# Transposing the merged branches of a decoder layer: fp32 transposes on TensorE against a split first and fp32r matmuls of 128 columns

## The chip, the cores and the metric

The kernel runs on one core of a Trainium2 chip. The metric is device time in microseconds (us), taken as the median of three runs. All times below are us unless ns is written.

## The reference

One layer of a decoder trunk, with 256 positions of 2048 channels. Three branches of width 1024 are computed from the normed input, gated, projected to 2048 channels and merged; a last projection and a norm follow. What matters here is the end of it:

```python
    ys = jnp.stack([y_a, y_b, y_x], axis=2)
    branch = jnp.einsum('bsnc,ncd->bsnd', ys, w_branch)
    gates = jax.nn.sigmoid(gate_logits.reshape(bsz, seq, N_BRANCH, D_MODEL))
    merged = jnp.sum(gates * branch, axis=2)
    out = merged @ w_out
    return x + rms_norm(out, post_g)
```

Inputs and outputs are fp32. The sizes in this part: `y_b` is 256 x 1024, `w_branch` of one branch 1024 x 2048, `merged` 256 x 2048, `w_out` 2048 x 2048.

## The kernel before, in words

Every large product is made from two fp32r parts of each operand: a high part (the value rounded to fp32r) and a low part (the rest). `split_to(hi, lo, src)` (L92 to L94) makes them: ScalarE (ACT) casts the source to the high part (L93), VectorE (DVE) subtracts that from the source (L94). Three matmuls then stand for one: high x high, high x low, low x high (`tm_mm`, L181 to L184). Weights come by DMA in tiles `raw` of 128 x 2048 and are split in halves of 128 x 1024 into `hl`, of which there are four buffers; so the split of one half waits until TensorE (PE) is done with the half four before it.

`tm_quarter` (L220) is the loop over one such tile: for each of its two halves it splits the weights, issues 12 matmuls of 512 columns (2 rows of K x 2 blocks of 128 tokens `tb` x 3 products) and then calls `pump`. PE's order is the order of the program text; DVE and ACT are ordered by a scheduler, and the weight splits carry a priority that puts them ahead. Background work lives in generators in the list `bg[2]`. Each `pump` advances each of them to its next `yield None`.

The place of the change is the last branch, B. The loop at L946 goes over `c`, four chunks of 512 channels of the merged result `mg` (two tiles M, one for each block of 128 tokens, tokens on partitions). A chunk has 4 halves of 12 matmuls into `Bp`. After that DVE multiplies `Bp` by the gate (L952, tile H) and adds it to `mg` (L953, tile M), and `merge_t(c)` (L931) is put in the background. The output projection needs `merged` with channels on partitions, as the stationary operand, so `merge_t` transposes the chunk: it passes two pumps, and then for each half `hf` of the chunk PE makes four transposes (L939: 2 blocks of 128 channels x 2 blocks of tokens) into the PSUM tile `mt`, and at the next pump `split_to` (L942) writes the high and low parts from `mt` to `mm_tile(c)`: ACT casts from PSUM, DVE subtracts from PSUM. Tile `mm_tile(c)` takes the slots H2, H3, U and X0 in turn, which a profile shows as H, U and X. The eight groups of transposes so fall two to a chunk, between the halves of the next chunk and, for the last, between the halves of the first block of the output projection (L973).

`pe.transpose(out, in_, ident)` is a matmul in transpose mode: the data is the stationary operand, the fp32 identity of 128 columns moves.

Of the kernel before, what the change touches and what calls it, by code (L numbers as in the profile page):

```python
# [9 lines left out]
F32 = mybir.dt.float32  # L10
F32R = mybir.dt.float32r
# [7 lines left out]
P = 128  # L19
D = 2048  # L20
T = 256
# [23 lines left out]
def trunk(ctx: ExitStack, tc: tile.TileContext, I, out):  # L45
    nc = tc.nc
    v, a, g, pe = nc.vector, nc.scalar, nc.gpsimd, nc.tensor
# [7 lines left out]
    wk = ctx.enter_context(tc.tile_pool(name="wk", bufs=2))  # L55
# [3 lines left out]
    bup = ctx.enter_context(tc.tile_pool(name="bup", bufs=2, space=PSUM))  # L59
    yp = ctx.enter_context(tc.tile_pool(name="yp", bufs=1, space=PSUM))  # L60
    miscp = ctx.enter_context(tc.tile_pool(name="miscp", bufs=1, space=PSUM))
# [4 lines left out]
    def nm(s):  # L66
        n_[0] += 1
        return f"{s}_{n_[0]}"

    def slot(tag, shape, dt=F32):  # L70
        return big.tile(shape, dt, tag=tag, name=nm(tag))
# [20 lines left out]
    def split_to(hi, lo, src):  # L92
        a.copy(out=hi, in_=src)  # L93
        v.tensor_tensor(out=lo, in0=src, in1=hi.bitcast(F32), op=ALU.subtract)  # L94
# [180 lines left out]
    ident = const.tile([P, P], F32, name="ident")  # L275
# [493 lines left out]
    mg = None  # L769
# [18 lines left out]
    def csl(c):  # L788
        return slice(c * 512, (c + 1) * 512)
# [18 lines left out]
    mg = Lazy()  # L808
# [97 lines left out]
    for bp in range(4):  # L906
# [12 lines left out]
        for i in range(2):  # L919
            d = yB[2 * bp + i]  # L920
# [5 lines left out]
    def mm_tile(i):  # L926
        if i not in mm:
            mm[i] = slot(("H2", "H3", "U", "X0")[i], [P, 4, 2, T], F32R)
        return mm[i]

    def merge_t(c):  # L931
        yield None
        yield None
        for hf in range(2):
            tp = miscp.tile([P, 2, T], F32, tag="misc", name=nm("mt"))
            for i in range(2):
                db = c * 4 + hf * 2 + i
                for tb in range(2):
                    pe.transpose(tp[:, i, tb * P:(tb + 1) * P], mg[tb][:, db * P:(db + 1) * P], ident)  # L939
            yield None  # L940
            d = mm_tile(c)[:, 2 * hf:2 * hf + 2]
            split_to(d[:, :, 0], d[:, :, 1], tp)  # L942
            if hf == 0:
                yield None

    for c in range(4):  # L946
        Bp = acc_tile()
        for kq in range(2):
            tm_quarter([Bp[:, 0], Bp[:, 1]], load(I["w_br"][1, c, kq]), yBs, kq, 8)
        for tb in range(2):  # L950
            d = sgB[tb][:, csl(c)]
            v.tensor_tensor(out=d, in0=Bp[:, tb], in1=d, op=ALU.mult)  # L952
            v.tensor_tensor(out=mg[tb][:, csl(c)], in0=mg[tb][:, csl(c)], in1=d, op=ALU.add)  # L953
        bg[2].append(merge_t(c))
# [65 lines left out]
    for tb in range(2):  # L1020
# [3 lines left out]
        c = slice(tb, tb + 1)  # L1024
# [107 lines left out]
```

## Time and profile before

| | |
|---|---|
| device time, median of 3 runs (lowest to highest) | 917.44 us (916.76 to 918.68) |
| the profiled execution, its own time | 916.64 us |
| its span, first to last instruction | 914.9 us |
| PE busy in the span | 902.5 us (99%) |
| DVE busy | 776.6 us (85%) |
| ACT busy | 535.6 us (59%) |
| mean granted clock of PE | 0.999 of full speed |

PE means TensorE's matmuls, PEld its weight loads, which run beside matmuls. A row names line, engine and operation, then out<-in with partitions x elements. Matmuls are pipelined: a row's duration (about 0.38 us for 512 columns) is longer than the step from its start to the start of the next (0.22 us), and what a matmul costs in a stream is that step. An fp32 operation is recorded as `f32` whether it is plain fp32 or fp32r on PE. A plain fp32 matmul shows as two records, a transpose or an fp32r matmul as one.

### The profile page before, as it was taken

The numbers are of one execution on the slowest core, as the hardware profiler recorded it, in microseconds if no ns is written. First come the engines' busy times: TensorE is split into PE (matmuls) and PEld (weight loads), VectorE is DVE, ScalarE is ACT, GpSimd is POOL, SyncE is SP. The second block draws the span as 40 slices with busy tenths as digits, with TensorE's granted clock in tenths as the row PEclk, the third lists the DMA queues.
The fourth block names the chain that finished last, engine by engine and source line by source line (L and its number), as shares of the span: only waits on it lengthen the run. The fifth ranks groups of instructions, "written<-read, shape, count | busy, mean of one in ns | idle before, by whom it ended". The sixth has DMA issues, their size and how long they took to land. (4 is left out here: it accounts for less than half of the span.)

```text
span 914.9 us, 13213 instructions
## 1 busy us (share of the span) xinstructions
PE 902.5 (99%) x4992; PEld 802.5 (88%) x4992; DVE 776.6 (85%) x1324; ACT 535.6 (59%) x865; POOL 22.1 (2%) x46
## 2 busy tenths in 40 slices
PE   9999999999999999999999999999999999999996
PEld 7999998899888888888899888888888888998896
DVE  7899957986779999999897799999998977876554
ACT  8576555665456657475554566555765646544452
POOL 1000000000000000000000000000000000000000
PEclk9999999999999999999999999999999999999999
DMA  9888565556355566655655545556466566657542
GB/s 358 312 318 297 196 226 191 193 190 230 138 190 190 195 223 221 220 204 185 230 190 184 198 184 194 196 200 226 158 234 229 176 207 227 218 184 277 192 177 92
DMA packets 30465, 193.35 MB, mean 211 GB/s; under 512 B 3905, under 2 KB 4417, under 8 KB 8641
## 3 DMA queue, kind: packets, MB, share of 16 engines
q1 hardware_dynamic: 28288, 186.18, 56.7%
q0 software_dynamic: 1536, 4.20, 1.4%
q10 hardware_dynamic: 576, 2.12, 0.6%
q8 instruction: 39, 0.64, 0.3%
q14 instruction: 26, 0.21, 0.1%
HBM read 190.39 MB, written 2.10 MB: 210 GB/s over the span
## 5 line engine op out<-in xcount | busy, mean ns | idle before, releaser
L94 DVE TENSOR_TENSOR hl<-raw,hl 128x1024 fp32r<-128x1024 f32 x319 | 388.1, 1219 | 101.2 <-ACT hl L93 98.1
L93 ACT CAST hl<-raw 128x1024 fp32r<-128x1024 f32 x319 | 329.5, 1045 | 179.9 <-PE acc L184 113.6
L172 PE MATMUL acc<-x,hl 128*128 128x512 f32 x736 | 241.5, 382 | 0.5 <-DVE x L166 0.5
L171 PE MATMUL acc<-x,hl 128*128 128x256 f32 x690 | 189.6, 275 | 0.8 <-DVE hl L94 0.6
L182 PE MATMUL acc<-hl,x 128*128 128x512 f32 x448 | 171.4, 383 | 0.0
L183 PE MATMUL acc<-hl,x 128*128 128x512 f32 x448 | 169.8, 379 | 0.0
L184 PE MATMUL acc<-hl,x 128*128 128x512 f32 x448 | 169.8, 379 | 0.0
L172 PEld LDWEIGHTS acc<-x,hl 128*128 128x128 f32 x736 | 136.8, 189 | 18.4 <-ACT hl L93 1.2
L171 PEld LDWEIGHTS acc<-x,hl 128*128 128x128 f32 x690 | 132.3, 192 | 3.5 <-DVE hl L94 2.4
L182 PEld LDWEIGHTS acc<-hl,x 128*128 128x128 f32 x448 | 84.7, 189 | 13.7 <-issue 2.5
L184 PEld LDWEIGHTS acc<-hl,x 128*128 128x128 f32 x448 | 84.7, 189 | 12.0
L183 PEld LDWEIGHTS acc<-hl,x 128*128 128x128 f32 x448 | 84.7, 189 | 11.3
L182 PE MATMUL acc<-hl,H 128*128 128x512 f32 (+1 forms) x224 | 83.5, 373 | 0.0
L183 PE MATMUL acc<-hl,H 128*128 128x512 f32 (+1 forms) x224 | 83.3, 372 | 0.0
L184 PE MATMUL acc<-hl,H 128*128 128x512 f32 (+1 forms) x224 | 83.2, 372 | 0.0
L183 PEld LDWEIGHTS acc<-hl,H 128*128 128x128 f32 x224 | 42.4, 189 | 5.6 <-DVE hl L94 0.2
L184 PEld LDWEIGHTS acc<-hl,H 128*128 128x128 f32 x224 | 42.4, 189 | 5.5
L182 PEld LDWEIGHTS acc<-hl,H 128*128 128x128 f32 x224 | 42.4, 189 | 5.3
L372 DVE TENSOR_TENSOR p<-p,E 128x512 f32<-128x512 f32 x64 | 44.1, 689 | 1.0
L600 DVE TENSOR_TENSOR_SCAN p<-s5r,p 128x256 f32<-128x256 f32 x64 | 42.5, 683 | 0.9
L372 DVE TENSOR_TENSOR p<-bu,E 128x512 f32<-128x512 f32 x64 | 41.3, 682 | 2.2 <-PE bu L561 2.2
L541 ACT COPY E<-ebase 128x64 f32<-128x64 f32 x32 | 7.7, 245 | 54.1 <-DVE p L372 52.2
(249 smaller groups left out, 1278.4 us busy)
## 6 DMA issues: line engine op xcount, KB each, us to landing
raw<-w_gate SPq DMA_DIRECT2D x48, 1024.0 KB, 4.7
raw<-w_br SPq DMA_DIRECT2D x24, 1024.0 KB, 4.7
raw<-w_out SPq DMA_DIRECT2D x16, 1024.0 KB, 4.7
raw<-w_xq SPq DMA_DIRECT2D x8, 1024.0 KB, 5.1
raw<-wk SPq DMA_DIRECT2D x8, 1024.0 KB, 4.9
raw<-wv SPq DMA_DIRECT2D x8, 1024.0 KB, 4.8
raw<-w_xg SPq DMA_DIRECT2D x8, 1024.0 KB, 4.7
raw<-w_av SPq DMA_DIRECT2D x8, 1024.0 KB, 4.7
```

Of the source, the lines that this page charges most:

```text
L93: a.copy(out=hi, in_=src)
L94: v.tensor_tensor(out=lo, in0=src, in1=hi.bitcast(F32), op=ALU.subtract)
L171: pe.matmul(ps[:, 0:T], lhsT=wl, rhs=hl.moving(0), start=False, stop=False)
L172: pe.matmul(ps, lhsT=wh, rhs=hl.moving_both(), start=first, stop=last)
L182: pe.matmul(ps, lhsT=hl.stationary(0, tb), rhs=two(wh), start=first, stop=False)
L183: pe.matmul(ps, lhsT=hl.stationary(0, tb), rhs=two(wl), start=False, stop=False)
L184: pe.matmul(ps, lhsT=hl.stationary(1, tb), rhs=two(wh), start=False, stop=last)
L372: v.tensor_tensor(out=o, in0=i0, in1=i1, op=op)
L541: a.copy(out=E[:, :, HT:HT + NB], in_=base[:, q])
L600: v.tensor_tensor_scan(out=p2[:, ri], data0=rb, data1=p1[:, ri], initial=0.0, op0=ALU.mult, op1=ALU.add)
```

## The change

`merge_t` splits first and transposes afterwards. When the chunk is merged, `split_to` makes the high and low parts of the 128 x 512 slice for each block of tokens, tokens on partitions, in a new tile `m2` (tag w0). After two pumps PE transposes both parts with plain `pe.matmul`, the data stationary in fp32r and an fp32r copy of the identity (`identr`, made once by ACT) moving, 128 columns: eight matmuls for each half `hf` of the chunk, the high parts into one PSUM tile, the low parts into another. Both come from the pool `bup` (2 buffers), which the kernel before uses for the state-space part and for the last output block, instead of `miscp` (1 buffer). At the next pump ACT copies the first tile to the high part of `mm_tile(c)` and DVE copies the second to the low part.

```diff
+    identr = wk.tile([P, P], F32R, tag="w2", name="identr", padded_shape=[P, 2 * P])
+    a.copy(out=identr, in_=ident)
+
     def merge_t(c):
+        ms_ = []
+        for tb in range(2):
+            m2 = wk.tile([P, 2, 512], F32R, tag="w0", name=nm("m2"))
+            split_to(m2[:, 0], m2[:, 1], mg[tb][:, csl(c)])
+            ms_.append(m2)
         yield None
         yield None
         for hf in range(2):
-            tp = miscp.tile([P, 2, T], F32, tag="misc", name=nm("mt"))
-            for i in range(2):
-                db = c * 4 + hf * 2 + i
-                for tb in range(2):
-                    pe.transpose(tp[:, i, tb * P:(tb + 1) * P], mg[tb][:, db * P:(db + 1) * P], ident)
+            d = mm_tile(c)[:, 2 * hf:2 * hf + 2]
+            tps = []
+            for z in range(2):
+                tp = bup.tile([P, 2, T], F32, tag="bu", name=nm("mt"))
+                for i in range(2):
+                    db = hf * 2 + i
+                    for tb in range(2):
+                        pe.matmul(tp[:, i, tb * P:(tb + 1) * P], lhsT=ms_[tb][:, z, db * P:(db + 1) * P], rhs=identr,
+                                  start=True, stop=True)
+                tps.append(tp)
             yield None
-            d = mm_tile(c)[:, 2 * hf:2 * hf + 2]
-            split_to(d[:, :, 0], d[:, :, 1], tp)
+            a.copy(out=d[:, :, 0], in_=tps[0])
+            v.tensor_copy(out=d[:, :, 1], in_=tps[1])
             if hf == 0:
                 yield None
```

The order of PE at the first group, which transposes the first half of chunk 0 between the third and the fourth half of chunk 1. Before:

```order
L183 MATMUL acc_7532<-hl_7567,yB_7252 128x512
L184 MATMUL acc_7532<-hl_7567,yB_7252 128x512
L939 MATMUL mt_7582<-ident,M_294_2727 128x128
L939 MATMUL mt_7582<-ident,M_295_2729 128x128
L939 MATMUL mt_7582<-ident,M_294_2727 128x128
L939 MATMUL mt_7582<-ident,M_295_2729 128x128
L182 MATMUL acc_7532<-hl_7587,yB_7253 128x512
```

With the change (`m_986` and `m_987` are the two split tiles):

```order
L183 MATMUL acc_7534<-hl_7575,yB_7252 128x512
L184 MATMUL acc_7534<-hl_7575,yB_7252 128x512
L950 MATMUL mt_7591<-identr,m_986_7552 128x128
L950 MATMUL mt_7591<-identr,m_987_7555 128x128
L950 MATMUL mt_7591<-identr,m_986_7552 128x128
L950 MATMUL mt_7591<-identr,m_987_7555 128x128
L950 MATMUL mt_7596<-identr,m_986_7552 128x128
L950 MATMUL mt_7596<-identr,m_987_7555 128x128
L950 MATMUL mt_7596<-identr,m_986_7552 128x128
L950 MATMUL mt_7596<-identr,m_987_7555 128x128
L182 MATMUL acc_7534<-hl_7601,yB_7253 128x512
```

The group keeps its place and has eight matmuls where it had four.

The order of DVE after chunk 0, where the merged result is written and, with the change, split. Before:

```order
L952 TENSOR_TENSOR H_837_6471<-acc_7463,H_837_6471 128x512
L94 TENSOR_TENSOR hl_7587<-raw_7565,hl_7587 128x1024
L953 TENSOR_TENSOR M_294_2727<-M_294_2727,H_836_6470 128x512
L953 TENSOR_TENSOR M_295_2729<-M_295_2729,H_837_6471 128x512
L94 TENSOR_TENSOR hl_7612<-raw_7610,hl_7612 128x1024
L94 TENSOR_TENSOR hl_7632<-raw_7610,hl_7632 128x1024
L94 TENSOR_TENSOR hl_7651<-raw_7649,hl_7651 128x1024
L94 TENSOR_TENSOR H_991_7602<-mt_7582,H_991_7602 128x2x256
```

With the change:

```order
L965 TENSOR_TENSOR H_837_6471<-acc_7465,H_837_6471 128x512
L94 TENSOR_TENSOR hl_7601<-raw_7573,hl_7601 128x1024
L966 TENSOR_TENSOR M_294_2727<-M_294_2727,H_836_6470 128x512
L966 TENSOR_TENSOR M_295_2729<-M_295_2729,H_837_6471 128x512
L94 TENSOR_TENSOR hl_7625<-raw_7623,hl_7625 128x1024
L94 TENSOR_TENSOR m_986_7552<-M_294_2727,m_986_7552 128x512
L94 TENSOR_TENSOR m_987_7555<-M_295_2729,m_987_7555 128x512
L94 TENSOR_TENSOR hl_7656<-raw_7623,hl_7656 128x1024
L94 TENSOR_TENSOR hl_7675<-raw_7673,hl_7675 128x1024
L955 CAST H_991_7590<-mt_7596 128x2x256
```

Two subtractions of 128 x 512 stand between two weight splits, and the subtraction that read `mt` has become a cast. ACT's casts of `m` stand in the same place of its own order.

## Rows read from the trace of the kernel before

**Rows 1.** The page: busy time of the engines, share of the span, instructions; and the granted clock in 40 equal slices of the span.

```profile
PE 902.5 (99%) x4992; PEld 802.5 (88%) x4992; DVE 776.6 (85%) x1324; ACT 535.6 (59%) x865; POOL 22.1 (2%) x46
PEclk9999999999999999999999999999999999999999
```

**Rows 2.** Busy time in the stretch from 786.4 to 842.4, which holds the eight groups of transposes. Columns: busy us and instructions of each engine, PE's granted clock, DMA share, GB/s.

```profile
786.40:842.40 56.00, 56.00 (x277) 50.20 (x276) 39.11 (x45) 25.50 (x29) 0.00 (x0) 1.00 0.62 226
```

**Rows 3.** The chain of work that ended last, in the same stretch: start, length, what. By line the transposes are 6.2% of it.

```profile
by line: PE acc L184 31.6%; PE acc L182 31.3%; PE acc L183 31.2%; PE mt L939 6.2%
796.55 0.44 PE mt L939 x4
...
835.92 0.44 PE mt L939 x4
```

**Rows 4.** PE in order of time (start, length of the row, instructions) around the first and the last group of transposes; 30 matmuls of 512 columns start between 789.70 and 796.17, counting the one at 789.70.

```profile
789.70 0.38 PE L184 MATMUL acc<-hl,yB 128*128 128x512 f32 x1
...
796.17 0.38 PE L184 MATMUL acc<-hl,yB 128*128 128x512 f32 x1
796.39 0.60 PE L939 MATMUL mt<-ident,M 128*128 128x128 f32 x4
796.74 0.47 PE L182 MATMUL acc<-hl,yB 128*128 128x512 f32 x1
797.05 0.38 PE L183 MATMUL acc<-hl,yB 128*128 128x512 f32 x1
...
835.75 0.60 PE L939 MATMUL mt<-ident,M 128*128 128x128 f32 x4
```

**Rows 5.** PE in order of time where fp32r matmuls of 256 columns follow each other, each with its own weight load (L177 to L179); 20 steps lie between the two rows.

```profile
90.73 0.28 PE L177 MATMUL acc<-H,hl 128*128 128x256 f32 x1
...
92.97 0.28 PE L179 MATMUL acc<-H,hl 128*128 128x256 f32 x1
```

**Rows 6.** PE in order of time: four plain fp32 matmuls of 128 columns, outside of transpose mode (L857, two records each), behind a pair of 256 and 512 columns.

```profile
462.50 0.27 PE L171 MATMUL acc<-x,hl 128*128 128x256 f32 x1
462.61 0.38 PE L172 MATMUL acc<-x,hl 128*128 128x512 f32 x1
462.83 1.05 PE L857 MATMUL z<-H,H 128*128 128x128 f32 x8
463.64 0.36 PE L171 MATMUL acc<-x,hl 128*128 128x256 f32 x1
463.83 0.38 PE L172 MATMUL acc<-x,hl 128*128 128x512 f32 x1
```

**Rows 7.** PE in order of time: four transposes whose stationary operand is read with a stride of two elements (L735, `p[:, qb, mb::2]`).

```profile
188.49 0.63 PE L735 MATMUL tp<-ident,p 128*128 128x128 f32 x4
188.88 0.46 PE L172 MATMUL acc<-x,hl 128*128 128x512 f32 x1
189.18 0.27 PE L174 MATMUL acc<-x,hl 128*128 128x256 f32 x1
```

**Rows 8.** Groups of weight loads, shapes kept apart: busy us, mean ns of one. L182 and L178 load fp32r, L857 plain fp32, L625 32 columns, L939 and L735 the data to be transposed.

```profile
L182 PEld LDWEIGHTS acc<-hl,H 128*128 128x128 f32 x224 | 42.4, 189 | 5.3
L178 PEld LDWEIGHTS acc<-H,hl 128*128 128x128 f32 x128 | 24.6, 192 | 0.0
L857 PEld LDWEIGHTS z<-H,H 128*128 128x128 f32 x32 | 4.2, 192 | 0.1
L939 PEld LDWEIGHTS mt<-ident,M 128*128 128x128 f32 x32 | 4.0, 141 | 0.8
L625 PEld LDWEIGHTS y<-s,cb 128*32 128x32 f32 x128 | 3.3, 109 | 3.9 <-issue 2.6
L735 PEld LDWEIGHTS tp<-ident,p 128*128 128x128 f32 x16 | 2.5, 200 | 0.0
```

**Rows 9.** Who waited for whom in the stretch from 786.4 to 842.4: us in total, times, longest.

```profile
ACT hl L93 <- PE acc L184: 31.2, 21, 1.5
DVE hl L94 <- ACT hl L93: 14.9, 12, 1.4
DVE H L952 <- PE acc L184: 0.3, 1, 0.3
```

**Rows 10.** DVE and ACT in order of time from the end of chunk 0 to the first group of transposes and what follows it (start, length, instructions, idle time before).

```profile
791.15 1.28 DVE L953 TENSOR_TENSOR M<-M,H 128x512 f32<-128x512 f32 x2
792.49 1.23 DVE L94 TENSOR_TENSOR hl<-raw,hl 128x1024 fp32r<-128x1024 f32 x1
795.08 1.23 DVE L94 TENSOR_TENSOR hl<-raw,hl 128x1024 fp32r<-128x1024 f32 x1 [1.36 <-ACT hl L93]
797.66 1.23 DVE L94 TENSOR_TENSOR hl<-raw,hl 128x1024 fp32r<-128x1024 f32 x1 [1.36 <-ACT hl L93]
...
791.41 1.05 ACT L93 CAST hl<-raw 128x1024 fp32r<-128x1024 f32 x1 [1.54 <-PE acc L184]
794.00 1.05 ACT L93 CAST hl<-raw 128x1024 fp32r<-128x1024 f32 x1 [1.54 <-PE acc L184]
```

**Rows 11.** Groups of splits of 128 x 512, from SBUF (`hl<-H`) and from PSUM (`H<-mt`): busy us, mean ns of one.

```profile
L94 DVE TENSOR_TENSOR hl<-H,hl 128x512 fp32r<-128x512 f32 x8 | 5.4, 681 | 0.0
L93 ACT CAST hl<-H 128x512 fp32r<-128x512 f32 x8 | 4.8, 603 | 0.0
L94 DVE TENSOR_TENSOR H<-mt,H 128x512 fp32r<-128x512 f32 x4 | 2.7, 683 | 0.0
L93 ACT CAST H<-mt 128x512 fp32r<-128x512 f32 x4 | 2.3, 578 | 0.0
```

## The prediction

> **What bounds the kernel now.** I first read the page's busy times: PE is busy 99% of the span, DVE 85%, ACT 59%, and the granted clock is full in all slices [rows 1]. A share of 99% says PE is the suspect, not that every instruction on it counts, so I went to the stretch of the change. From 786.4 to 842.4 PE is busy for all 56.00 us, DVE for 39.11 and ACT for 25.50 [rows 2], and the chain that ended last is there made of PE alone, the transposes 6.2% of it, in eight pieces of 0.44 us [rows 3]. The waits say the same from the other side: ACT's weight splits wait 31.2 us for PE to release a buffer, DVE's wait 14.9 us for ACT, and PE is in no row as the one that waits [rows 9]. So any time put on PE here is added to the kernel, and any time put on DVE and ACT is free until PE has to wait for it.
>
> The next thing to read is what a matmul costs in this stream. Not its duration: a transpose lasts 273 ns by its record, but four of them and a 512-column matmul pass from 796.39 to 797.05, in 0.66 us [rows 4]. Between 789.70 and 796.17 lie 30 steps of a 512-column matmul, 0.2157 each. So a group of four transposes costs 0.66 - 0.216 = 0.44. A longer base gives it better: first and last group start at 796.39 and 835.75, seven periods of 5.623, each with 24 matmuls of 512 columns (5.177); what is left is 0.446 for a group, 0.1115 for one transpose.
>
> **What is removed.** 32 transposes in 8 groups, 8 x 0.446 = 3.57 us of PE, all on the path.
>
> **What is added on PE.** 64 fp32r matmuls of 128 columns, each with a weight load of 128 x 128. The trace has no fp32r matmul under 256 columns, so its price is bounded. From below: in a pair of 256 and 512 columns the 256 take one step of 0.11 [rows 6], so 128 columns that only stream would take half of it, 0.055; nothing excludes that from the side of the columns, but a matmul can't be cheaper than its stream. From above: a plain fp32 matmul of 128 columns outside of transpose mode takes two records. Eight records and one of 256 columns fill 462.83 to 463.83, so a record is (1.00 - 0.11) / 8 = 0.111 and the matmul 0.223 [rows 6].
>
> Between these I take the weight load as the limit. Where fp32r matmuls of 256 columns follow each other, 20 steps take 2.24 us, 0.112 each [rows 5], where in a pair, with a longer matmul to hide the load, they take 0.11 [rows 6]: as dear, or a touch dearer. A load of 128 columns lasts 189 to 192 ns, one of 32 columns 109 [rows 8]: 96 columns more cost 80 to 83 ns, so 128 columns occupy some 0.11 us of the load path, with a latency on top. That loads can set the step is seen at the other transposes: those of L735 have the same shape as ours, but their strided loads take 200 ns instead of 141 [rows 8], and four of them cost 189.18 - 188.49 - 0.216 = 0.47, so 0.118 each instead of 0.1115 [rows 7]. The new loads are contiguous fp32r, like L178, so I take 0.1115: half as many columns, the same step. 64 x 0.1115 = 7.14 us.
>
> The sum on PE is 7.14 - 3.57 = **+3.57 us**: the work is doubled and the single piece stays as dear as it was. With the step between 0.109 and 0.118 it is 3.4 to 4.0.
>
> The skill speaks against leaving transpose mode at all: the Trainium skill, "TensorE: Matmul & The Clock Gate", section Terms, calls this mode four times faster for FP32. Taken as a rule for these matmuls it would make each 4 x 0.1115 and add 25 us. The trace disagrees even for plain fp32, where the factor is 0.223 / 0.1115 = 2 [rows 4, 6], and the sum goes by the rows.
>
> **What is added on DVE and ACT.** Per chunk DVE gains two subtractions of 128 x 512 from SBUF at 0.68; its two subtractions from PSUM become casts from PSUM, for which the old 0.68 is the nearest row. ACT gains two casts of 0.60 and keeps two copies of 0.58 [rows 11]. Over four chunks DVE goes from 39.1 to 44.5, ACT from 25.5 to 30.3, in a stretch that PE stretches from 56.0 to 59.6. I cost this at nothing; the cover is DVE's idle time behind ACT (1.36 before a weight split [rows 10]) and the four weight buffers. If the cover were gone, up to 5.4 us of DVE work would stand before weight splits.
>
> **The new wait.** PE's groups now wait for the splits. DVE has the merged chunk at 792.43, then a weight split to 793.72, then the two new subtractions to about 795.08, just where the next weight split starts today [rows 10], so that one isn't delayed. ACT is free at 792.46 and done with both casts by 793.66, before its next weight split at 794.00. PE wants the high parts at 796.17 (load one step ahead) and the low parts four matmuls later, at about 796.6 [rows 4]. The slack is 2.5 and 1.5 us. Behind a waiting load stand all further matmuls. The identity is copied once, long before. The copies out of PSUM have the same two pumps as before, and no longer depend on each other; the two `bup` buffers are wanted again only a period of 5.6 us later. No DMA is added or moved past another.
>
> **The number.** The profiled execution took 916.64 us (span 914.9), 0.8 under the median. It should become 920.2; from the median, 917.44 + 3.57 = **921.0 us**. With the bounds of the step and the spread of the runs (0.7 below to 1.2 above) this case gives 920.1 to 922.7. A measurement tells about 0.2%, 1.8 us, from no change, so this is a small but clear loss.
>
> **Rivals.**
>
> *The load path is not the limit (no change).* If fp32r loads can overlap more than these rows show, 128 columns go at their stream, at best 0.055: 64 x 0.055 = 3.52, a difference of -0.05, 917.4. For it: no row has a load behind a shorter matmul. Against: the 0.112 of [rows 5] and the 0.118 of [rows 7], where the step is longer than the columns need. It decides for "same" when the step is under about 0.083 (919.2). I give 0.13, half on each side of that. The Trainium skill, "TensorE: Matmul & The Clock Gate", section Back-to-back issue gap, gives about 81 ns for a stream of loads and matmuls of 128 columns. By it the estimate is 64 x 0.081 - 3.57 = +1.6, 919.1; no run here shows it, as its loads would have to be faster than those of [rows 8].
>
> *Small fp32r matmuls are as dear as fp32.* Then each costs 0.216 to 0.223, the price of 512 columns or of a plain fp32 matmul of 128: +10.3 to +10.7, 927.7 to 928.1. For it: no row under 256 columns in fp32r. Against: 256 and 512 columns of fp32r go at one price per column, without a sign of a fixed cost [rows 4, 5]. Chance 0.10.
>
> *The split comes late.* If DVE takes the next weight split before the two subtractions, they end at 795.08 + 1.23 + 1.36 = 797.67, some 1.0 us after PE wants the low parts, at each of four chunks: 4 us more, 925. It decides when they slip by over 1.5 us. Against: the order has them ahead of that split. Chance 0.09.
>
> That is 0.66 for the forecast, 0.13, 0.10, 0.09, and 0.02 for a gain that no row explains. The range 919.0 to 926.0 holds the forecast, the late split and the nearer half of the first rival: 0.66 + 0.09 + 0.06 = 0.81. Slower by over 0.2%: 0.66 + 0.10 + 0.09 + 0.06 = 0.91; within it 0.07; faster 0.02.
>
> **What would show it.** A group of eight should take 0.89 us from its first start, less the step of the 512 that closes it, where four took 0.446; the period between groups should go from 5.62 to 6.07. The loads of L950 should last 189 to 192 ns, not 141. The clock should stay full, PE should have no idle in the stretch, and the splits of `m` should end before 796. A group of 0.45 would mean the first rival, one of 1.7 the second, and PE idle ahead of L950 with DVE as releaser the third. A time off by more than 1.5 us with groups of 0.89 would mean something outside of `merge_t`, and my sum would be wrong in its cover.

## The result and the profile after

The changed kernel takes 920.96 us (median of 6 runs, 920.76 to 921.85) against 917.96 of the kernel before in the same count of runs. The ratio is 1.0037, with a 95% interval of 1.0027 to 1.0047: slower by 2.5 to 4.3 us (the medians alone are 3.0 apart). The forecast was 921.0 with a range of 919.0 to 926.0.

The page of the changed kernel: busy time of the engines and the granted clock, to be read beside [rows 1].

```profile
PE 906.8 (99%) x5024; PEld 806.6 (88%) x5024; DVE 781.4 (85%) x1332; ACT 539.9 (59%) x874; POOL 22.0 (2%) x46
PEclk9999999999999999999999999999999999999998
```

PE has 32 records more and 4.3 us of busy time more. The granted clock is the same but for the last slice, 8 tenths for 9; there PE runs out of work, its last matmul ending 7.9 us before the end in both kernels. DVE and ACT have grown by 4.8 and 4.3 us. That the numbers are alike means nothing; the chain says which of them counts. The chain of work that ended last, in the stretch from 786 to 846, beside [rows 3]:

```profile
by line: PE acc L182 29.9%; PE acc L183 29.5%; PE acc L184 29.5%; PE mt L950 11.2%
797.37 0.84 PE mt L950 x8
...
839.94 0.84 PE mt L950 x8
```

It is still PE alone, and the share of the transposing matmuls has gone from 6.2% to 11.2%. PE in order of time around the first and the last group, beside [rows 4]:

```profile
796.99 0.38 PE L184 MATMUL acc<-hl,yB 128*128 128x512 f32 x1
797.21 1.00 PE L950 MATMUL mt<-identr,m 128*128 128x128 f32 x8
798.05 0.44 PE L182 MATMUL acc<-hl,yB 128*128 128x512 f32 x1
798.33 0.38 PE L183 MATMUL acc<-hl,yB 128*128 128x512 f32 x1
...
839.77 1.00 PE L950 MATMUL mt<-identr,m 128*128 128x128 f32 x8
```

Eight matmuls and one of 512 columns pass from 797.21 to 798.33. Less 0.216 for the 512, a group costs 0.904. The long base says the same: (839.77 - 797.21) / 7 = 6.080 a period, less 5.177 for 24 matmuls of 512 columns, is 0.903. One matmul's share of the price is 0.113. (The eight starts alone fill 797.21 to 798.05, 0.105 each; the rest of the price is that the 512-column matmul behind them takes 0.28 to its successor instead of 0.216.) The weight loads of these matmuls, beside those of [rows 8]:

```profile
L950 PEld LDWEIGHTS mt<-identr,m 128*128 128x128 f32 x64 | 8.4, 191 | 0.4
```

They last 191 ns on average, like the fp32r loads of [rows 8] (189 to 192), where the transposes' loads lasted 141. The waits from 786.4 to 846.4, beside [rows 9], have no row in which PE waits, and neither have those of any run below:

```profile
ACT hl L93 <- PE acc L184: 30.7, 21, 2.0
DVE hl L94 <- ACT hl L93: 12.5, 12, 1.7
DVE H L965 <- PE acc L184: 1.9, 4, 0.5
```

And DVE in order of time before the first group, beside [rows 10]: the two new subtractions fill the gap in which DVE had waited for ACT.

```profile
791.98 1.29 DVE L966 TENSOR_TENSOR M<-M,H 128x512 f32<-128x512 f32 x2
793.31 1.23 DVE L94 TENSOR_TENSOR hl<-raw,hl 128x1024 fp32r<-128x1024 f32 x1
794.45 1.29 DVE L94 TENSOR_TENSOR m<-M,m 128x512 fp32r<-128x512 f32 x2
795.90 1.23 DVE L94 TENSOR_TENSOR hl<-raw,hl 128x1024 fp32r<-128x1024 f32 x1 [0.16 <-ACT hl L93]
```

The idle time before the next weight split has shrunk from 1.36 to 0.16 us. The low parts are there at 795.74. The first load of the group starts with the matmul at 796.99, and the low parts are wanted four matmuls later.

One thing has to be kept out of the comparison: the span of this profiled execution is 919.4 against 914.9, 4.5 longer. Of that, 0.8 lies before the change begins to act: the first group starts 0.82 later than before. In the first 14 us ACT waited 0.6 longer for loads of the input; the rows there are, before and after:

```profile
ACT x L165 <- DMA st<-start: 0.9, 3, 0.4
```

```profile
ACT x L165 <- DMA st<-start: 1.5, 2, 1.2
```

The code there is the same in both, and I take this for the spread between executions: in the traces of the runs below the first group starts anywhere from 796.77 to 798.69. From the first group on the difference is 3.66 = 8 x 0.457, which is the change.

### The profile page after: what moved, and what is told of

Its sections match the earlier page's. It is cut to its first block, busy times and chain, and to the rows that moved or that the text cites. A ratio compares the mean times of both kernels' runs of the same rounds, so it can differ in the third digit from the quotient of the medians.

```text
span 919.4 us, 13303 instructions
## 1 busy us (share of the span) xinstructions
PE 906.8 (99%) x5024; PEld 806.6 (88%) x5024; DVE 781.4 (85%) x1332; ACT 539.9 (59%) x874; POOL 22.0 (2%) x46
## 5 line engine op out<-in xcount | busy, mean ns | idle before, releaser
L182 PE MATMUL acc<-hl,x 128*128 128x512 f32 x448 | 171.4, 383 | 0.0
L182 PEld LDWEIGHTS acc<-hl,x 128*128 128x128 f32 x448 | 84.7, 189 | 13.7 <-issue 2.5
L182 PE MATMUL acc<-hl,H 128*128 128x512 f32 (+1 forms) x224 | 83.4, 373 | 0.0
L182 PEld LDWEIGHTS acc<-hl,H 128*128 128x128 f32 x224 | 42.4, 189 | 5.3
```

The lines of the kernel that those rows point to most:

```text
L182: pe.matmul(ps, lhsT=hl.stationary(0, tb), rhs=two(wh), start=first, stop=False)
```

## The experiments

The theory: PE's own work is the whole loss; each fp32r matmul of 128 columns costs one weight load, 0.112, and half as many columns gain nothing. The rivals: short fp32r matmuls have a price of their own; or part of the loss is the new work on DVE and ACT. A group's price is read in each run as above, from the row of the group to the second matmul behind it, less 0.216. Starts are shown to 0.01 us, so such a price is uncertain by about 0.01 (the kernel before gives 0.444 so, and 0.447 over the seven periods of [rows 3]).

**Half a load.** Stationary operand of 64 columns, POOL fills the channels that are left out.

```diff
-                        pe.matmul(tp[:, i, tb * P:(tb + 1) * P], lhsT=ms_[tb][:, z, db * P:(db + 1) * P], rhs=identr,
+                        pe.matmul(tp[0:64, i, tb * P:(tb + 1) * P], lhsT=ms_[tb][:, z, db * P:db * P + 64], rhs=identr,
                                   start=True, stop=True)
...
-            a.copy(out=d[:, :, 0], in_=tps[0])
-            v.tensor_copy(out=d[:, :, 1], in_=tps[1])
+            g.memset(d[64:P].bitcast(F32), 0.0)
+            a.copy(out=d[0:64, :, 0], in_=tps[0][0:64])
+            v.tensor_copy(out=d[0:64, :, 1], in_=tps[1][0:64])
```

> The changed kernel with a weight load of 64 columns in place of 128 for each of the 64 matmuls (the transposed copy of the other 64 channels of each block is left out and filled with zeros by POOL). Moving columns stay at 128. Theory that the load path sets the step: a load of half the columns takes about 0.055, the step of the eight matmuls falls from 0.113 to 0.055 to 0.065, a group from 0.91 to about 0.5, and the time by 8 x 0.4 = 3.2, to about 917.8, near the kernel before. Rival, that short fp32r matmuls have a price of their own (half the rate under 256 columns, or a floor): step 0.11, group 0.9, time 921.0 as with the change.

Measured: 918.96 us, ratio to the kernel before 1.0011 (1.0002 to 1.0020). PE in order of time:

```profile
798.34 0.64 PE L950 MATMUL mt<-identr,m 128*64 128x128 f32 x8
798.82 0.44 PE L182 MATMUL acc<-hl,yB 128*128 128x512 f32 x1
799.10 0.38 PE L183 MATMUL acc<-hl,yB 128*128 128x512 f32 x1
```

The group costs 799.10 - 798.34 - 0.216 = 0.54 instead of 0.90, and eight starts fill 798.34 to 798.82, 0.06 each where the change has 0.105. So a matmul of 128 fp32r columns has no floor at 0.11: with a shorter load it goes at 0.06. That is the theory's side, if a little above the expectation in the group (0.5) and in the time (917.8). The loads:

```profile
L950 PEld LDWEIGHTS mt<-identr,m 128*64 128x64 f32 x64 | 5.1, 135 | 0.8
```

64 columns less take 191 - 135 = 56 ns off the record, so 128 columns are worth an estimated 112 ns: the step of the change. Half a load also halves what a matmul writes to PSUM; the next run does that too, and gains nothing by it.

**Half the moving columns.** 64 columns of the identity, loads as with the change; POOL fills the tokens that are left out.

```diff
-                        pe.matmul(tp[:, i, tb * P:(tb + 1) * P], lhsT=ms_[tb][:, z, db * P:(db + 1) * P], rhs=identr,
+                        pe.matmul(tp[:, i, tb * P:tb * P + 64], lhsT=ms_[tb][:, z, db * P:(db + 1) * P], rhs=identr[:, 0:64],
                                   start=True, stop=True)
...
```

> The changed kernel with 64 moving columns in place of 128 (half of the identity; the other tokens of each block are left out and filled with zeros by POOL). The weight loads stay at 128 columns. Theory that the load path sets the step: step 0.11, group 0.9, time 921.0, nothing gained by half the columns. Rival, that the columns set it at half the rate of long matmuls: step 0.055, group 0.45, time about 917.5.

Measured: 920.9 us, ratio 1.0038 (1.0025 to 1.0051), as with the change.

```profile
796.87 0.97 PE L950 MATMUL mt<-identr,m 128*128 128x64 f32 x8
797.67 0.47 PE L182 MATMUL acc<-hl,yB 128*128 128x512 f32 x1
797.98 0.38 PE L183 MATMUL acc<-hl,yB 128*128 128x512 f32 x1
```

The group costs 0.894, so nothing is gained by half the columns.

**Twice the moving columns.** The identity beside zeros, 256 columns, the two token blocks summed in PSUM.

```diff
...
-                        pe.matmul(tp[:, i, tb * P:(tb + 1) * P], lhsT=ms_[tb][:, z, db * P:(db + 1) * P], rhs=identr,
-                                  start=True, stop=True)
+                        pe.matmul(tp[:, i, :], lhsT=ms_[tb][:, z, db * P:(db + 1) * P],
+                                  rhs=identr[:, 1 - tb:3 - tb, :], start=tb == 0, stop=tb == 1)
```

> The changed kernel with 256 moving columns in each of the 64 matmuls (the identity beside zeros, the two token blocks added up in PSUM): twice the columns, the same loads. Theory that the load path sets the step at up to 256 columns: step 0.112, group 0.9, time 921.0, nothing lost by twice the columns. Rival, that the columns count in any part: step up to 0.22, time up to 928.

Measured: 921.09 us, ratio 1.0036 (1.0022 to 1.0049).

```profile
796.77 1.12 PE L951 MATMUL mt<-identr,m 128*128 128x256 f32 x8
797.73 0.38 PE L182 MATMUL acc<-hl,yB 128*128 128x512 f32 x1
797.94 0.38 PE L183 MATMUL acc<-hl,yB 128*128 128x512 f32 x1
```

The group costs 0.954. Four times the columns of the run before raise it by 7%. Together the three runs show that the load sets the step: half the load takes a matmul's share of the price from 0.113 to 0.068, while 64, 128 and 256 columns give 0.112, 0.113 and 0.119.

**The split alone.** The kernel before with DVE's and ACT's new splits added, unused.

```diff
     def merge_t(c):
+        for tb in range(2):
+            m2 = wk.tile([P, 2, 512], F32R, tag="w0", name=nm("m2"))
+            split_to(m2[:, 0], m2[:, 1], mg[tb][:, csl(c)])
         yield None
```

> The kernel before, with the split of the merged chunk on DVE and ACT added and not used; the transposes are those of before. DVE gets 5.5 us of work more in this stretch, ACT 4.9. Theory that all of this is under cover: as before, 918.0, within 0.6, and no wait of PE in the stretch. Rival, that part of the loss comes from DVE and ACT and their weight splits: up to 3 us over before, with PE idle ahead of L182 to L184 in the stretch.

Measured: 917.43 us, ratio 1.0001 (0.9992 to 1.0009). The group as before:

```profile
798.00 0.60 PE L942 MATMUL mt<-ident,M 128*128 128x128 f32 x4
798.36 0.47 PE L182 MATMUL acc<-hl,yB 128*128 128x512 f32 x1
798.67 0.38 PE L183 MATMUL acc<-hl,yB 128*128 128x512 f32 x1
```

798.67 - 798.00 - 0.216 = 0.454, within the rounding of before, and no row of the waits has PE in it. The cover holds, to within 0.8 us.

**High parts alone.** Half of the changed kernel's matmuls; the low part is a second copy of the high one.

```diff
-            for z in range(2):
+            for z in range(1):
...
-            v.tensor_copy(out=d[:, :, 1], in_=tps[1])
+            v.tensor_copy(out=d[:, :, 1], in_=tps[0])
```

> The changed kernel with the high parts alone transposed, 32 fp32r matmuls in place of 64; the low part is copied from the same PSUM tile, so DVE and ACT do as much as with the change. Theory that a transpose costs the same step in either form and only the count matters: group 0.45, period of groups 5.62, time as before, 918.0, within 0.6. Rival, that the fp32r form has a cost of its own beside the count (a turn from one form to the other, or the waits on the split): over before by 1 us or more.

Measured: 918.06 us, ratio 1.0002 (0.9993 to 1.0011).

```profile
797.73 0.56 PE L950 MATMUL mt<-identr,m 128*128 128x128 f32 x4
798.13 0.44 PE L182 MATMUL acc<-hl,yB 128*128 128x512 f32 x1
798.40 0.38 PE L183 MATMUL acc<-hl,yB 128*128 128x512 f32 x1
```

Four fp32r matmuls cost 0.454, within 0.01 of four fp32 transposes, with as much work on DVE and ACT as with the change. The loss is the count.

**The old transposes with half a load.** The other half of the channels is filled by POOL. This is to see whether they cost the same as the new matmuls for the same reason.

```diff
-                    pe.transpose(tp[:, i, tb * P:(tb + 1) * P], mg[tb][:, db * P:(db + 1) * P], ident)
+                    pe.transpose(tp[0:64, i, tb * P:(tb + 1) * P], mg[tb][:, db * P:db * P + 64], ident)
...
```

> The kernel before, its 32 fp32 transposes with a load of 64 columns in place of 128 (the other 64 channels of each block are left out and filled with zeros by POOL). Theory: an fp32 transpose is bound by its moving columns, at two units each, not by its load, so the step stays 0.109, group 0.44, time 918.0. Rival: these too are bound by the load: step 0.055, group 0.25, time 916.4.

Measured: 917.47 us, ratio 0.9997 (0.9988 to 1.0007).

```profile
796.83 0.60 PE L939 MATMUL mt<-ident,M 128*64 128x128 f32 x4
797.19 0.47 PE L182 MATMUL acc<-hl,yB 128*128 128x512 f32 x1
797.49 0.38 PE L183 MATMUL acc<-hl,yB 128*128 128x512 f32 x1
```

The group stays at 0.444. The fp32 transpose isn't held by its load. The 0.111 a record in [rows 6] can't say whether it is held by its columns, as each of those records has a load of 128 columns too. Plain fp32 matmuls of 256 columns in the kernel before can:

```profile
178.91 1.89 PE L714 MATMUL sc<-M,X 128*128 128x256 f32 x8
180.44 0.46 PE L171 MATMUL acc<-x,hl 128*128 128x256 f32 x1
180.74 0.38 PE L172 MATMUL acc<-x,hl 128*128 128x512 f32 x1
```

Eight records and one fp32r matmul of 256 columns fill 178.91 to 180.74, so a record of 256 fp32 columns takes (1.83 - 0.11) / 8 = 0.215, twice what 256 fp32r columns take, and 128 of them an estimated 0.108. The 0.109 of the transposes fits that. So the two forms seem to meet at 0.11 by coincidence, one by its columns, the other by its load; no run varies the columns of the fp32 transposes.

**The change in transpose mode.** The same 64 pieces, fp32r, with `pe.transpose`.

```diff
-                tp = bup.tile([P, 2, T], F32, tag="bu", name=nm("mt"))
+                tp = bup.tile([P, 2, T], F32R, tag="bu", name=nm("mt"))
...
-                        pe.matmul(tp[:, i, tb * P:(tb + 1) * P], lhsT=ms_[tb][:, z, db * P:(db + 1) * P], rhs=identr,
-                                  start=True, stop=True)
+                        pe.transpose(tp[:, i, tb * P:(tb + 1) * P], ms_[tb][:, z, db * P:(db + 1) * P], identr)
...
```

> The changed kernel with its 64 matmuls in transpose mode on the fp32r parts (PSUM tile fp32r). The loads of transposes lasted 141 ns before, those of the change 189 to 192. Theory: the load path sets the step of the change, and transpose mode loads about twice as fast, so the step falls to what 128 columns need, about 0.06, a group to about 0.52, the time to about 918.2, the loss nearly gone. Rival: fp32r in transpose mode moves at the fp32 transposes' rate (0.109): group 0.9, time 921.0.

Measured: 920.04 us, ratio 1.0020 (1.0011 to 1.0029). Loads, then PE in order of time:

```profile
L950 PEld LDWEIGHTS mt<-identr,m 128*128 128x128 f32 x64 | 6.3, 140 | 0.8
```

```profile
798.69 0.80 PE L950 MATMUL mt<-identr,m 128*128 128x128 f32 x8
799.33 0.46 PE L182 MATMUL acc<-hl,yB 128*128 128x512 f32 x1
799.62 0.38 PE L183 MATMUL acc<-hl,yB 128*128 128x512 f32 x1
```

The loads take 140 ns as expected, but the group costs 0.714, not 0.52, and eight starts fill 0.64, 0.08 each. My expectation missed: transpose mode gives back less than half of the loss. The loads of one group in order of time, with the change and here:

```profile
797.00 1.07 PEld L950 LDWEIGHTS mt<-identr,m 128*128 128x128 f32 x8
```

```profile
798.48 0.87 PEld L950 LDWEIGHTS mt<-identr,m 128*128 128x128 f32 x8
```

The first load has a whole 512-column matmul to itself. From the second on, the single loads in the trace start 0.109 to 0.112 apart with the change and 0.082 to 0.091 apart here, while the first two matmuls of a group here are 0.06 to 0.07 apart and the later ones fall into the loads' step. So the load seems to be the limit here too, at 0.085 and not at the 0.06 that I took from the duration of its record. That is read from the starts; no run varies the load in this mode.

**The low part in bf16.** A second piece of type bf16 in place of the low fp32r one, with a bf16 identity; the low part has fewer bits.

```diff
...
-            m2 = wk.tile([P, 2, 512], F32R, tag="w0", name=nm("m2"))
-            split_to(m2[:, 0], m2[:, 1], mg[tb][:, csl(c)])
+            m2 = wk.tile([P, 512], F32R, tag="w0", name=nm("m2"), padded_shape=[P, 1024])
+            m3 = wk.tile([P, 512], BF16, tag="w1", name=nm("m3"), padded_shape=[P, 1024])
+            split_to(m2, m3, mg[tb][:, csl(c)])
...
-                        pe.matmul(tp[:, i, tb * P:(tb + 1) * P], lhsT=ms_[tb][:, z, db * P:(db + 1) * P], rhs=identr,
+                        pe.matmul(tp[:, i, tb * P:(tb + 1) * P], lhsT=ms_[tb][z][:, db * P:(db + 1) * P], rhs=idents[z],
```

> The changed kernel with the low part kept and transposed in bf16 (bf16 identity), so 32 of the 64 loads are bf16, like the warm-up's at 140 ns; the low part loses bits. Theory that the load path sets the step: fp32r 0.112 and bf16 about 0.06, group 4 x 0.112 + 4 x 0.06 = 0.69, time about 918 + 8 x (0.69 - 0.447) = 919.9, a good 1 us under the change. Rival, that each matmul of 128 columns costs 0.11 whatever its type: 921.0.

Measured: 919.99 us, ratio 1.0020 (1.0011 to 1.0028). Loads by type, then PE in order of time:

```profile
L954 PEld LDWEIGHTS mt<-identr,m 128*128 128x128 f32 x32 | 4.8, 191 | 0.4
L954 PEld LDWEIGHTS <-m 128*128 128x128 bf16 x32 | 1.8, 98 | 0.0
```

```profile
797.15 0.56 PE L954 MATMUL mt<-identr,m 128*128 128x128 f32 x4
797.55 0.40 PE L954 MATMUL mt<-identb,m 128*128 128x128 bf16 x4
797.76 0.47 PE L182 MATMUL acc<-hl,yB 128*128 128x512 f32 x1
798.07 0.38 PE L183 MATMUL acc<-hl,yB 128*128 128x512 f32 x1
```

The group costs 0.70, as expected: four fp32r matmuls fill 797.15 to 797.55, 0.10 each, and the rest of the group, four bf16 ones, takes 0.30: their starts fill 797.55 to 797.76, 0.05 each, and the rest is the turn back to fp32r. The same 128 columns are cheaper where the load is shorter, here by type and not by leaving data out; the moving identity changes its type as well.

**All groups in one table.** Eight times a group's price, less eight times 0.447, against the measured ratio as a difference at 918 us. The fourth column is uncertain by about 0.1.

| run | matmuls in a group | group, us | 8 x (group - 0.447) | measured, us (95%) |
|---|---|---|---|---|
| the change | 8 | 0.904 | 3.7 | 3.4 (2.5 to 4.3) |
| half a load | 8 | 0.54 | 0.7 | 1.0 (0.2 to 1.8) |
| half the columns | 8 | 0.894 | 3.6 | 3.5 (2.3 to 4.7) |
| twice the columns | 8 | 0.954 | 4.1 | 3.3 (2.0 to 4.5) |
| split alone | 4 | 0.454 | 0.1 | 0.1 (-0.7 to 0.8) |
| high parts alone | 4 | 0.454 | 0.1 | 0.2 (-0.6 to 1.0) |
| old ones, half a load | 4 | 0.444 | 0.0 | -0.3 (-1.1 to 0.6) |
| transpose mode, fp32r | 8 | 0.714 | 2.1 | 1.8 (1.0 to 2.7) |
| low part in bf16 | 8 | 0.70 | 2.0 | 1.8 (1.0 to 2.6) |

PE's price of a group accounts for each of the nine times, within its interval. None of them is clearly faster than the kernel before.

## Why the prediction was right

- *PE is the bound in this stretch.* Right, and for the reason given: no PE wait in the rows, and the nine times follow PE's price alone.
- *The 32 transposes cost 0.1115 each.* Right: four of them are the group of 0.447 in the kernel before. The reason stood open. It is not their loads, as the run with half a load shows; that it is their columns is argued from the price of other fp32 columns. The prediction had read the 0.118 at L735 as loads setting the step of transposes. For contiguous data they don't, and whether the strided loads of L735 do is not tested.
- *The 64 new matmuls cost 0.1115 each.* 0.113 measured; 64 x 0.113 = 7.23 for the 7.14 of the sum. The reason, the load path, was argued from loads of 189 to 192 ns and a step of 0.112 in [rows 5, 8]; it is now shown by half a load against half and twice the columns. Of the two premises only the first was good: 256 columns take 0.11 even where a longer matmul hides their load [rows 6], so the 0.112 of [rows 5] could not tell one from the other.
- *No gain in half as many columns.* The rival of a step at the columns' own rate was wrong, but not because that rate is out of reach: with half a load, matmuls of 128 columns do go at 0.06. The bottom of the bound was real, and the load lies above it. The 0.081 that the same rival priced isn't seen for these matmuls either.
- *Short fp32r matmuls as dear as fp32.* Wrong: no floor, as the same run shows.
- *The rule on transpose mode.* The factor of four that the Trainium skill, "TensorE: Matmul & The Clock Gate", section Terms, gives for FP32 doesn't appear for fp32r: a group costs 0.904 against 0.714 in transpose mode, a factor of 1.3. Its warning was right in sign, and the trace points to the loads, which last 140 ns there and not 191.
- *Cover on DVE and ACT.* Right in the sum: the added split alone gives 0.1 us (-0.7 to 0.8). The slack of the low parts was 1.5 by the forecast; in the trace they are ready at 795.74, with the group's first start at 797.21 and their own turn four matmuls later.
- *The number.* 3.57 of the sum against 3.66 from the first group on, and 3.4 (2.5 to 4.3) in the runs. The signs that it named are there too: a group of 0.904 for 0.89, a period of 6.08 for 6.07, loads of 191 ns, no wait of PE.

## What to carry to other kernels

Where PE is busy without a gap, price a short matmul by the longer of two things, its columns and its weight load. Take the price of the load from steps between matmuls that wait for it, in the same type and mode. For plain matmuls with 128 columns of fp32r to load it is the load, and fewer than 256 moving columns save next to nothing. A split that is moved ahead of a transpose doubles the transposes, and a second engine's saved dependence buys nothing while PE does not wait for it. Read the cost as the step between starts, never as a record's duration: 273 ns and 0.11 us were the same matmul, 140 ns and about 0.085 us the same load.

## What was not expected of the hardware

- Transpose mode on fp32r lies between: loads of 140 ns as in fp32, but 0.08 us from start to start, under the 0.105 of plain fp32r matmuls and over the 0.06 of 128 fp32r columns with half a load. The starts of the loads point to the load as its limit; it is not tested.
- Equal prices seem to have come from different limits. Halving the load took an fp32r matmul's share of the price from 0.113 to 0.068 and left an fp32 transpose at 0.11.
- bf16 loads of 128 columns lasted 98 ns in a stream, where the expectation had taken the 140 of the warm-up; fp32r ones lasted 191.
